# Seventeen SwiGLU pairs from seven block products: a decoder layer in split f32 on one core

## The chip, the cores and the metric

The kernel runs on one core of one Trainium2 chip. The metric is the device time of one execution in microseconds; the time of a kernel is the median of its runs. All times below are microseconds unless marked ns.

## The reference, cut to what matters

One layer (DEPTH = 1) of a decoder with D_MODEL = 1024 over 1024 prompt tokens and 32 sample tokens (8 sequences of 4), which share the weights. Two branches (a gated linear recurrence and a chunked linear attention) are merged and projected, and then comes a SwiGLU feed-forward network with D_FF = 2816, which the change touches:

```python
m = sigmoid(u_ga) * (y_a @ proj_a) + sigmoid(u_gb) * (y_b @ proj_b)
x = x + gt1 * (m @ w_out)
h2 = rmsnorm(x, norm2_g) * (1.0 + sc2) + sh2
f1, f2 = split(h2 @ ffn_w1, 2, axis=-1)          # 1024 -> 2 x 2816
x = x + gt2 * ((silu(f1) * f2) @ ffn_w2)         # 2816 -> 1024
```

All data is float32, and the result has to have float32's precision.

## The kernel before, in words

*Halves.* Half A is 512 prompt tokens; half B is the other 512 and the 32 sample tokens, 544 columns. Activations lie with features on the 128 partitions and tokens along the free axis. In half B every product is worked in two parts of 272 columns, each in its own PSUM bank of a two-bank tile from `mm(...)`.

*Split float32.* TensorE multiplies in the reduced format fp32r, so each operand is held as a high and a low part, and each 128x128 block of weights takes three matmuls: high by high (L355), high by low (L356), low by high (L357). For activations, `split` makes both parts: ACT copies the high part, DVE subtracts it. For weights, `load_raw` issues a transfer on SP's queue into a `raw` buffer (3 of them), and `split_w` splits it into an `hl` buffer (3 of them): ACT's copy L136, then DVE's subtraction L137. A split of 1024 columns serves 8 blocks.

*The feed-forward network.* D_FF is worked as 22 rows of 128 features. `pair(f, part, a)` makes one: tile `f1` (gate, 512 KB of weights, 8 blocks) and tile `f2` (value, another 512 KB), in half B 2 x 8 x 3 x 2 = 96 matmuls of 128x272. ACT takes tanh of half the gate (L1093), DVE multiplies it out (L1094, L1097), ACT and DVE split the product (L1099, L1100) into the tile `fa`, from which `ffn2` makes the output. Group 0 is pairs 0 to 10, group 1 pairs 11 to 21; `ffn2(0)` comes after group 0, `ffn2(1)` after group 1. In each half, pairs 0 to 3 are worked early, one part at a time, and from pair 4 on a pair does both parts.

*Order.* Half A runs through its branches, its attention output, second norm and FFN group 0 (all inside `branches`, the last steps in `back`), then `A.ffn1(1)` and `A.ffn2(1)`, into which half B's first norm is mixed; then half B's branches and FFN. Within that, a scheduler sets each engine's order from dependences and from priorities: what is written under `tc.high_priority(n)` goes up by n places. `split_w` has 70 (`AHEAD`). Each engine takes its instructions in its own order and waits on semaphores for the others. GpSimd (POOL) has some products of the attention, small copies of states (`hist`, `hlast`) and the issue of the output transfers (`out_ya`, `out_yb`); in the FFN it has nothing else. The tile of the tag `m2t` (one buffer of 128 x 1088) serves the recurrence of half A and then that of half B.

In the trace, tiles of half A end in `a`, those of half B in `b`: `f1psb11None` is the PSUM tile of pair 11's gate in half B.

Of the kernel before, what the change touches and what calls it, by code (L numbers as in the profile page):

```python
# [15 lines left out]
P = 128  # L16
# [4 lines left out]
NF = 22  # L21
# [6 lines left out]
LEVELS = (64, 32, 16, 8, 4, 2, 1)  # L28
EPS = 1e-6
EARLY = 4  # L30
AHEAD = 70
def starts_of(w):
    return [min(i, w - P) for i in range(0, w, P)]
# [14 lines left out]
def hybrid_layer(ctx, tc, I, O):  # L48
    nc = tc.nc
    pe, act, dve, pool, sp = nc.tensor, nc.scalar, nc.vector, nc.gpsimd, nc.sync  # L50
# [12 lines left out]
    wp = ctx.enter_context(tc.tile_pool(name="wp", bufs=3))  # L63
# [23 lines left out]
    def mm(name):  # L87
        return mmk[1].tile([P, mmk[0], 512], F32, tag="mm", name=name)
# [36 lines left out]
    def load_raw(src, n, name):  # L125
        raw = wp.tile([P, 1024], F32, tag="raw", name=name + "_raw")
        sp.dma_start(raw[:, :n], src)
        return raw

    def load_w(src, n, name):  # L130
        return split_w(load_raw(src, n, name), n, name)

    def split_w(raw, n, name):
        hl = wp.tile([P, 2, 1024], F32R, tag="hl", name=name + "_hl", bufs=3)
        with tc.high_priority(AHEAD):
            act.activation(hl[:, 0, :n], raw[:, :n], AF.Copy)  # L136
            dve.tensor_sub(hl[:, 1, :n], raw[:, :n], hl[:, 0, :n].bitcast(F32))  # L137
        return hl

    held = {}  # L140
# [17 lines left out]
    class Apart:  # L158
        def __init__(s, *of):
            s.of = of  # L160

        def __getitem__(s, at):
            rows, u, cols = at
            return s.of[u][rows, cols]

    def w_in_tile(t, name):
        return load_w(I["w_in"][t], 1024, name)

    def split(dst, src, n):
        act.activation(dst[:, 0:n], src, AF.Copy)  # L170
        dve.tensor_sub(dst[:, n:2 * n], src, dst[:, 0:n].bitcast(F32))
# [68 lines left out]
    def ada_rest():  # L240
        for cc in range(4, 12):
            yield from ada_chunk(cc)
# [45 lines left out]
    def drain(g):  # L288
        for _ in g:
            pass  # L290
# [15 lines left out]
    def mix(main, fill):  # L306
        credit = 0.0
        for want in main:
            credit = min(credit, 3.0) - want
            while credit < 0:  # L310
                got = next(fill, None)
                if got is None:
                    break
                credit += got

    class Half:
        def __init__(s, hf):
            s.hf, s.N = hf, WID[hf]
            s.n = "ab"[hf]

            s.whole = (0, s.N, None, None)
            s.parts = [(0, 256, 0, 0), (256, 256, 0, 256)] if hf == 0 else [(0, 272, 0, 0), (272, 272, 1, 0)]
            s.adas = ada_rest() if hf == 0 else iter(())
            s.early = {}
            s.lr_raw = None

        def ada(s, n):
# [728 lines left out]
        def out_proj(s, part, acc):  # L1056
            o, w = part[0], part[1]
            for q in range(KD):
# [21 lines left out]
        def pair(s, f, part, a):  # L1080
# [14 lines left out]
            p2 = mm("f2ps" + n)  # L1095
            s.gemm(p2, load_kept(("f2", f), I["ffn1"][2 * f + 1], 1024, "f2" + n, fr and f >= EARLY - 2), 8, s.h2, part=gp)
            dve.tensor_mul(ti(tg), ti(tg), s.psv(p2, part))  # L1097
# [2 lines left out]
            dve.tensor_sub(lo, tg, hi.bitcast(F32))  # L1100
            yield w * 24 / 2400.0

        def ffn1_first(s, part, n):
            for f in range(n) if part[0] == 0 else range(n - 1, -1, -1):
                if part[0] == 0:
                    s.act.append(S(f"fa{s.n}{f}", F32R))
                yield from s.pair(f, part, s.act[f])

        def ffn1(s, g, f0=0):
            if f0 == 0:  # L1110
                s.act = []
            for f in range(11 * g + f0, 11 * g + 11):
                a = S(f"fa{s.n}{f}", F32R)
                yield from s.pair(f, s.whole, a)
                s.act.append(a)
# [33 lines left out]
        def back(s):  # L1149
            s.x, s.h2 = [], []  # L1150
            p0, p1 = s.parts
            a0, a1 = [ACC("20" + s.n)], [ACC("21" + s.n)]
            drain(s.out_proj(p0, a0))
            o1 = s.out_proj(p1, a1)
            next(o1)
            next(o1)
            mix(s.norm2(p0, a0), o1)
            drain(o1)
            s.act = []
            f = s.ffn1_first(p0, EARLY)  # L1160
            next(f)
            next(f)
            mix(s.norm2(p1, a1), f)
            drain(f)
            drain(s.ffn1_first(p1, EARLY))
            drain(s.ffn1(0, EARLY))
            drain(s.ffn2(0, s.whole))

        def branches(s, before):
# [37 lines left out]
    load_later()  # L1207
    derive()
    A.branches(None)
    up1 = A.ffn1(1)  # L1210
    for _ in range(16):
        next(up1)
# [113 lines left out]
```

## Time and profile before

| what | value |
|---|---|
| median of 3 runs | 2042.29 (2042.16 to 2043.36) |
| the profiled execution, its own time | 2041.18 |
| span of its records | 2039.2 |
| granted TensorE clock, mean | 0.996 |
| busy share of the span: PE, PEld, DVE, ACT, POOL | 98%, 89%, 54%, 39%, 4% |
| moved by DMA | 228.39 MB, 112 GB/s |
| share of the 16 DMA engines taken by SP's queue | 32.8% |

A row of the timeline gives the start, the duration, the engine, the source line, the operation with its output and inputs, and in brackets how long the engine had been idle before it and what ended that. A row of the windows gives the stretch and its length, then the busy time and the count of PE, PEld, DVE, ACT and POOL, then the granted clock, the busy share of the DMA engines and the GB/s. A row of the groups by line has busy time and mean; one of the waits has who waits, who ends the wait, and sum, count and longest wait. "DMA issues" lists count, KB and microseconds from issue to landing.

### The profile page before, as it was taken

How to read it: one execution, taken by the hardware profiler on the slowest of the kernel's cores; microseconds unless marked ns; L12 is line 12 of the kernel's file. 1: busy time of each engine (PE TensorE's matmuls, PEld its weight loads, DVE VectorE, ACT ScalarE, POOL GpSimd, SP SyncE). 2: the span in 40 equal slices, each digit the busy share in tenths (PEclk: the TensorE clock that was granted, in tenths of full speed). 3: DMA queues.
4: the chain of work that ended last, by engine and by line, in shares of the span. 5: the costliest groups of instructions: out<-in, count | busy, mean ns of one | idle time of the engine just before them, and what ended most of it. 6: DMA issues, size and time to landing. Idle time of an engine off the chain costs nothing. (4 is left out here: it accounts for less than half of the span.)

```text
span 2039.2 us, 31760 instructions
## 1 busy us (share of the span) xinstructions
PE 2005.9 (98%) x13306; PEld 1808.0 (89%) x13306; DVE 1096.8 (54%) x1768; ACT 799.0 (39%) x1117; POOL 76.1 (4%) x130
## 2 busy tenths in 40 slices
PE   8999999999999999999999999999999999999997
PEld 5887877777899888888899999999999999999997
DVE  5647586544358433446473597764334773333346
ACT  3534375533335322333352355653322442222232
POOL 0101001000000000000010011010000000000000
PEclk9999999999999999999999999999999999999998
DMA  8323223334344323232412312323233542232243
GB/s 305 105 92 125 88 94 116 102 119 159 93 153 158 124 78 119 93 132 84 149 63 87 126 53 94 109 89 104 73 92 108 177 134 87 72 105 93 82 121 123
DMA packets 74638, 228.39 MB, mean 112 GB/s; under 512 B 8704, under 2 KB 16768, under 8 KB 74496
## 3 DMA queue, kind: packets, MB, share of 16 engines
q1 hardware_dynamic: 71536, 217.38, 32.8%
q0 software_dynamic: 2416, 8.44, 1.1%
q8 instruction: 104, 1.70, 0.3%
q10 hardware_dynamic: 544, 0.56, 0.1%
q14 instruction: 38, 0.31, 0.0%
HBM read 217.11 MB, written 9.23 MB: 111 GB/s over the span
## 5 line engine op out<-in xcount | busy, mean ns | idle before, releaser
L357 PE MATMUL f3psb<-fab,f3b_hl 128*128 128x272 f32 x352 | 101.4, 288 | 0.0
L355 PE MATMUL f3psb<-fab,f3b_hl 128*128 128x272 f32 x352 | 101.3, 288 | 0.0
L356 PE MATMUL f3psb<-fab,f3b_hl 128*128 128x272 f32 x352 | 100.9, 287 | 0.0
L136 ACT ACTIVATE f3b_hl<-f3b_raw 128x768 fp32r<-128x768 f32 (+1 forms) x45 | 35.7, 793 | 88.6 <-PE f3psb L357 58.3
L355 PE MATMUL f3psa<-faa,f3a_hl 128*128 128x512 f32 x176 | 68.7, 390 | 0.0
L357 PE MATMUL f3psa<-faa,f3a_hl 128*128 128x512 f32 x176 | 68.5, 389 | 0.0
L356 PE MATMUL f3psa<-faa,f3a_hl 128*128 128x512 f32 x176 | 68.5, 389 | 0.0
L355 PEld LDWEIGHTS f3psb<-fab,f3b_hl 128*128 128x128 f32 x352 | 66.4, 189 | 0.0
L357 PEld LDWEIGHTS f3psb<-fab,f3b_hl 128*128 128x128 f32 x352 | 66.2, 188 | 0.0
L356 PEld LDWEIGHTS f3psb<-fab,f3b_hl 128*128 128x128 f32 x352 | 66.1, 188 | 0.0
L137 DVE TENSOR_TENSOR f3b_hl<-f3b_raw,f3b_hl 128x768 fp32r<-128x768 f32 (+1 forms) x45 | 40.1, 892 | 35.2 <-ACT f3b_hl L136 34.8
L136 ACT ACTIVATE f3a_hl<-f3a_raw 128x768 fp32r<-128x768 f32 (+1 forms) x32 | 25.4, 793 | 84.3 <-PE f3psa L357 47.9
L137 DVE TENSOR_TENSOR f3a_hl<-f3a_raw,f3a_hl 128x768 fp32r<-128x768 f32 (+1 forms) x32 | 28.5, 892 | 39.1 <-ACT f3a_hl L136 38.4
L355 PE MATMUL uxpsb<-h1b,uxpsb_hl 128*128 128x272 f32 x160 | 47.0, 293 | 0.1
L357 PE MATMUL uxpsb<-h1b,uxpsb_hl 128*128 128x272 f32 x160 | 46.4, 290 | 0.0
L355 PE MATMUL ugpsb<-h1b,ugpsb_hl 128*128 128x272 f32 x160 | 46.2, 289 | 0.0
L357 PE MATMUL ugpsb<-h1b,ugpsb_hl 128*128 128x272 f32 x160 | 46.1, 288 | 0.0
L356 PE MATMUL uxpsb<-h1b,uxpsb_hl 128*128 128x272 f32 x160 | 45.9, 287 | 0.0
L356 PE MATMUL ugpsb<-h1b,ugpsb_hl 128*128 128x272 f32 x160 | 45.8, 286 | 0.0
L357 PEld LDWEIGHTS f3psa<-faa,f3a_hl 128*128 128x128 f32 x176 | 33.0, 188 | 7.0 <-DVE f3a_hl L137 0.2
L356 PEld LDWEIGHTS f3psa<-faa,f3a_hl 128*128 128x128 f32 x176 | 33.0, 188 | 6.9
L355 PEld LDWEIGHTS f3psa<-faa,f3a_hl 128*128 128x128 f32 x176 | 33.0, 188 | 6.8
(1477 smaller groups left out, 7129.0 us busy)
## 6 DMA issues: line engine op xcount, KB each, us to landing
ada<-in_ada_w SPq DMA_DIRECT2D x48, 512.0 KB, 5.3
f3b_raw<-in_ffn SPq DMA_DIRECT2D x23, 384.0 KB, 3.1
f3b_raw<-in_ffn SPq DMA_DIRECT2D x22, 320.0 KB, 2.9
woa_raw<-in_w_out SPq DMA_DIRECT2D x13, 512.0 KB, 3.5
wob_raw<-in_w_out SPq DMA_DIRECT2D x13, 512.0 KB, 3.2
f3a_raw<-in_ffn SPq DMA_DIRECT2D x16, 384.0 KB, 3.1
uxpsa_raw<-in_w_in SPq DMA_DIRECT2D x10, 512.0 KB, 3.6
ugpsa_raw<-in_w_in SPq DMA_DIRECT2D x10, 512.0 KB, 3.6
```

Of the source, the lines that this page charges most:

```text
L136: act.activation(hl[:, 0, :n], raw[:, :n], AF.Copy)
L137: dve.tensor_sub(hl[:, 1, :n], raw[:, :n], hl[:, 0, :n].bitcast(F32))
L355: pe.matmul(out, wh, x[:, o:o + w], start=st, stop=False)
L356: pe.matmul(out, wh, x[:, N + o:N + o + w], start=False, stop=False)
L357: pe.matmul(out, wl, x[:, o:o + w], start=False, stop=en)
```

## The change

*Fewer products.* A pair of half B has two outputs (gate f1 and value f2) for two parts of 272 tokens, from two halves of the 1024 features (k-tiles 0 to 3 and 4 to 7): as blocks, a 2x2 matrix times a 2x2 matrix, eight block products of 4 blocks and 12 matmuls each. For pairs 5 to 21, `pair7` makes the four outputs from seven such products, after Strassen and Winograd, with sums of the weights on the one side and of the tokens on the other. With A0, A1 for the gate's weights and B0, B1 for the value's (0: k-tiles 0 to 3, 1: 4 to 7), and h for the first part's tokens:

- x = A0 h (tile `qa`, first 512 columns), and later, called x' here, A1 h is added to it in the same bank (`qa`, second half): the gate of the first part;
- y = d0 t2 and v = d2 t3 (tile `qc` holds d0 and d2);
- z = d3 t1, and B1 t4 is added to v (tile `qb` holds d3 and B1);
- d1 times the second part's k-tiles 4 to 7 is added to z (tile `qd`, only 512 wide).

d0 = A0+B0+B1, d1 = d0+A1, d2 = A0+B0, d3 = B0+B1. Results x and y share the PSUM tile `xy`, v and z the tile `wz`. Between the products, `e` is ACT's copy of x ahead of x', u2 = y - e (L1189), u4 = u2 + v (L1194); the value f2 of the second part is u4 - z (L1201), that of the first u2 + v (L1203), and the gate of the second part z - u2 (L1208). Its tanh (L1209), L1210, the product with f2 over 544 columns (L1211) and the split (L190, L191) finish the pair. Tiles `qa` and `qc` are split by ACT and DVE as before (now L137, L138); for `qb` and `qd` GpSimd subtracts the low part. A pair takes six transfers of 256 or 512 KB on SP's queue instead of two of 512 KB, and 84 matmuls instead of 96.

*The sums of the weights.* `make_sums` runs after half A's branches: for each of the 17 pairs two rounds on GpSimd, each with two loads of 256 KB on its own queue, four additions of 128x256, and a store of 512 KB into a DRAM tile `sum`. All rounds use the one buffer of the tag `m2t`.

*The sums of the tokens.* `mixed` runs in half B between pair 4 and pair 5: from h2's 8 tiles it makes t1 to t4, for each of four j eight DVE additions or subtractions of 272 or 544 columns and three splits. t1 takes the place of the second part in h2's tiles 0 to 3, the others have tiles of their own.

```diff
-    def split_w(raw, n, name):
+    def split_w(raw, n, name, eng=None):
...
-            dve.tensor_sub(hl[:, 1, :n], raw[:, :n], hl[:, 0, :n].bitcast(F32))
+            (eng or dve).tensor_sub(hl[:, 1, :n], raw[:, :n], hl[:, 0, :n].bitcast(F32))
...
+    def make_sums(fs):
+        for f in fs:
+            sums[f] = dp.tile([P, 4, 512], F32, tag=f"sum{f}", name=f"sum{f}")
+            for i in range(2):
+                q = tp.tile([P, 2 * 544], F32, tag="m2t", name=f"sq{f}{i}", bufs=1)[:, :1024].rearrange("p (s n) -> p s n", s=4)
+                c = slice(256 * i, 256 * i + 256)
+                for u in range(2):
+                    pool.dma_start(q[:, 2 * u:2 * u + 2, :], I["ffn1"][2 * f + u].rearrange("p (k n) -> p k n", k=2)[:, :, c])
+                pool.tensor_add(q[:, 3], q[:, 2], q[:, 3])
+                pool.tensor_add(q[:, 2], q[:, 0], q[:, 2])
+                pool.tensor_add(q[:, 0], q[:, 0], q[:, 3])
+                pool.tensor_add(q[:, 1], q[:, 1], q[:, 0])
+                pool.dma_start(sums[f][:, :, c], q)
...
+        def mixed(s):
+            N, w = s.N, s.N // 2
+            s.t1, s.t2, s.t3, s.t4 = [], [], [], []
+            for j in range(4):
+                n = f"{s.n}{j}"
+                h, g = s.h2[j], s.h2[4 + j]
+                hs, gs = T("mh" + n), T("mg" + n)
+                dve.tensor_add(hs[:, :N], h[:, :N].bitcast(F32), h[:, N:2 * N].bitcast(F32))
+                dve.tensor_add(gs[:, :N], g[:, :N].bitcast(F32), g[:, N:2 * N].bitcast(F32))
+                p, q = T("mp" + n), T("mq" + n)
+                dve.tensor_sub(p[:, :w], hs[:, :w], hs[:, w:N])
+                dve.tensor_add(p[:, w:N], p[:, :w], gs[:, w:N])
+                dve.tensor_sub(q[:, :w], hs[:, w:N], gs[:, w:N])
+                dve.tensor_sub(q[:, w:N], gs[:, :w], p[:, w:N])
+                t34 = S("mt" + n, F32R)
+                split(t34, q[:, :N], N)
...
+                split(t2[:, c:c + N], p[:, w:N], w)
...
+                hi, lo = h[:, w:N], h[:, N + w:2 * N]
+                act.activation(hi, p[:, :w], AF.Copy)
+                dve.tensor_sub(lo, p[:, :w], hi.bitcast(F32))
...
+        def pair7(s, f, a):
...
+            xy, wz = mm("xy" + n), mm("wz" + n)
+            x, y = (xy[:, 0, :w], xy[:, 1, :w]) if s.hf else (xy[:, 0, :w], xy[:, 0, w:N])
+            v, z = (wz[:, 0, :w], wz[:, 1, :w]) if s.hf else (wz[:, 0, :w], wz[:, 0, w:N])
...
+            ha = load_w(I["ffn1"][2 * f], 1024, "qa" + n)
+            prod(x, ha, 0, s.quarter(0, 0), True, True)
+            with tc.high_priority(AHEAD + 20):
+                act.activation(e, x, AF.Copy)
+            hc = load("qc", (d[:, 0], d[:, 2]))
+            prod(y, hc, 0, s.t2, True, True)
+            with tc.high_priority(AHEAD + 20):
+                dve.tensor_sub(u2, y, e)
+            prod(x, ha, 1, s.quarter(4, 0), False, True)
+            prod(v, hc, 1, s.t3, True, True)
+            with tc.high_priority(AHEAD + 20):
+                dve.tensor_add(u4, u2, v)
+            act.activation(tg[:, :w], x, AF.Tanh, scale=0.5)
+            dve.scalar_tensor_tensor(tg[:, :w], tg[:, :w], 1.0, x, op0=OP.add, op1=OP.mult)
+            hb = load("qb", (d[:, 3], I["ffn1"][2 * f + 1][:, 512:]), pool)
+            prod(z, hb, 0, s.t1, True, True)
+            with tc.high_priority(AHEAD + 20):
+                dve.tensor_sub(f2[:, w:N], u4, z)
+            prod(v, hb, 1, s.t4, False, True)
+            dve.tensor_add(f2[:, :w], u2, v)
+            hd = load("qd", (d[:, 1],), pool)
+            prod(z, hd, 0, s.quarter(4, 1), False, True)
+            with tc.high_priority(AHEAD + 20):
+                dve.tensor_sub(f12, z, u2)
+            act.activation(tg[:, w:N], f12, AF.Tanh, scale=0.5)
+            dve.scalar_tensor_tensor(tg[:, w:N], tg[:, w:N], 1.0, f12, op0=OP.add, op1=OP.mult)
+            dve.tensor_mul(tg[:, :N], tg[:, :N], f2[:, :N])
+            split(a, tg[:, :N], N)
...
-                yield from s.pair(f, s.whole, a)
+                yield from s.pair7(f, a) if s.seven and f >= PLAIN else s.pair(f, s.whole, a)
...
     A.branches(None)
+    make_sums(range(PLAIN, NF))
```

Lines of `pair7`, `mixed` and `make_sums` are counted in the changed kernel, where L355 to L357 of a seven-product pair are L1166 to L1168.

*How the order moves.* First TensorE in half B, at the seam in a pair: before, the last matmuls of pair 5's gate and the first of its value (`f1psb5None`, `f2psb5None`).

```order
L355 MATMUL f1psb5None_14851<-h2b_14088,f1b5None_hl 128x272
L356 MATMUL f1psb5None_14851<-h2b_14088,f1b5None_hl 128x272
L357 MATMUL f1psb5None_14851<-h2b_14088,f1b5None_hl 128x272
L355 MATMUL f2psb5None_14908<-h2b_13975,f2b5None_hl 128x272 [waits DVE_49,Activation_49]
L356 MATMUL f2psb5None_14908<-h2b_13975,f2b5None_hl 128x272
L357 MATMUL f2psb5None_14908<-h2b_13975,f2b5None_hl 128x272 [waits DVE_49]
```

After, the last matmul of y (weights `qc`, tokens `mu`, that is t2), the last of v's first product (tokens `mt`, t3), and the first five of x', for the pair after the first.

```order
L1168 MATMUL xyb_15338<-mub_15189,qcb_hl 128x272
L1168 MATMUL wzb_15339<-mtb_15204,qcb_hl 128x272
L1166 MATMUL xyb_15338<-h2b_14325,qab_hl 128x272 [waits DVE_49]
L1167 MATMUL xyb_15338<-h2b_14325,qab_hl 128x272
L1168 MATMUL xyb_15338<-h2b_14325,qab_hl 128x272
```

Before, TensorE waits here for the split of weights that has been asked for ahead; now x' goes into the tile of which y has just been written, and its first matmul waits for the DVE instruction that reads y, L1189. A product of the next pair (x) is also moved in between this pair's: the order of products is z of `qb`, half of the next x, v of t4, the other half but one matmul, z of `qd`, that matmul, v of t3, y and x'.

DVE at the same place, before: splits of weights (L137), and one pair's gating (L1094, L1097, L1100).

```order
L1100 TENSOR_TENSOR fab_14735<-ftb4None_14790,fab_14735 128x544
L1094 SCALAR_TENSOR_TENSOR ftb5None_14905<-ftb5None_14905,f1psb5None_14851 128x544
L137 TENSOR_TENSOR f2b6None_hl<-f2b6None_raw,f2b6None_hl 128x1024
L1097 TENSOR_TENSOR ftb5None_14905<-ftb5None_14905,f2psb5None_14908 128x544
L137 TENSOR_TENSOR f1b7None_hl<-f1b7None_raw,f1b7None_hl 128x1024
L1100 TENSOR_TENSOR fab_14850<-ftb5None_14905,fab_14850 128x544
```

After: the split of `qc`, the last steps of the pair before (tiles `vf`, `tg`, `ff`, `fa`; numbers 15211 to 15217), and u2 of this pair (`eu`, 15340).

```order
L138 TENSOR_TENSOR qcb_hl<-qcb_raw,qcb_hl 128x1024
L1208 TENSOR_TENSOR vfb_15215<-wzb_15213,eub_15214 128x272
L1210 SCALAR_TENSOR_TENSOR tgb_15216<-tgb_15216,vfb_15215 128x272
L1211 TENSOR_TENSOR tgb_15216<-tgb_15216,ffb_15217 128x544
L1189 TENSOR_TENSOR eub_15340<-xyb_15338,eub_15340 128x272
L191 TENSOR_TENSOR fab_15211<-tgb_15216,fab_15211 128x544
L1194 TENSOR_TENSOR vfb_15341<-eub_15340,wzb_15339 128x272
L138 TENSOR_TENSOR qab_hl<-qab_raw,qab_hl 128x1024
L1201 TENSOR_TENSOR ffb_15343<-vfb_15341,wzb_15339 128x272
```

L1189, for which x' waits, stands in DVE's queue behind L1208, L1210 and L1211 of the pair before, which follow z and ACT's tanh.

GpSimd in half A, before: the last copies of states, then the transfers of A's output.

```order
L899 COPY hist<-uba_3137 128x3
L953 COPY hlast<-laa_3239 128x1
L953 COPY hlast<-laa_3255 128x1
L1147 DMA out_ya<-ya_7652 128x1024
L1147 DMA out_ya<-ya_7656 128x1024
L1147 DMA out_ya<-ya_7660 128x1024
```

After, at the same place: the first round of sums (`sq` is the work buffer, `sum` the DRAM tile).

```order
L179 DMA sq_6273<-in_ffn 128x2x256
L974 COPY hlast<-laa_3241 128x1
L179 DMA sq_6273<-in_ffn 128x2x256
L974 COPY hlast<-laa_3257 128x1
L180 TENSOR_TENSOR sq_6273<-sq_6273 128x256
L181 TENSOR_TENSOR sq_6273<-sq_6273 128x256
L182 TENSOR_TENSOR sq_6273<-sq_6273 128x256
L183 TENSOR_TENSOR sq_6273<-sq_6273 128x256
L184 DMA sum_6272<-sq_6273 512x1x256
```

Thirty-three more rounds follow, and the transfers of `out_ya` stand behind the last store:

```order
L183 TENSOR_TENSOR sq_6553<-sq_6553 128x256
L184 DMA sum_6544<-sq_6553 512x1x256
L1259 DMA out_ya<-ya_7943 128x1024
L1259 DMA out_ya<-ya_7947 128x1024
L1259 DMA out_ya<-ya_7951 128x1024
```

More of the change, by code (lines that the diff above doesn't have):

```diff
@@ L30 @@
 EARLY = 4
+PLAIN = 5
 AHEAD = 70
@@ L164, in __getitem__ @@
             return s.of[u][rows, cols]
+    dp = ctx.enter_context(tc.tile_pool(name="dp", bufs=1, space=bass.MemoryType.DRAM))
+    sums = {}
+    def make_sums(fs):
[11 more added lines that the diff above has]
+                pool.dma_start(sums[f][:, :, c], q)
     def w_in_tile(t, name):
@@ L324, in __init__ @@
             s.early = {}
+            s.seven = s.hf == 1
             s.lr_raw = None
@@ new lines, in quarter, with prod, load @@
+        def quarter(s, k0, c):
+            N, w = s.N, s.N // 2
+            return [(h[:, c * w:c * w + w], h[:, N + c * w:N + c * w + w]) for h in s.h2[k0:k0 + 4]]
+        def pair7(s, f, a):
+            n, N, w = f"{s.n}{f}", s.N, s.N // 2
+            d = sums[f]
+            def prod(out, hl, u, rhs, first, last):
+                for k, (xh, xl) in enumerate(rhs):
+                    c = u * 512 + k * P
+                    wh, wl = hl[:, 0, c:c + P], hl[:, 1, c:c + P]
+                    pe.matmul(out, wh, xh, start=(first and k == 0), stop=False, skip_group_check=True)
+                    pe.matmul(out, wh, xl, start=False, stop=False, skip_group_check=True)
+                    pe.matmul(out, wl, xh, start=False, stop=(last and k == 3), skip_group_check=True)
+            def load(name, parts, eng=None):
+                raw = wp.tile([P, 1024], F32, tag="raw", name=name + n + "_raw")
+                for i, src in enumerate(parts):
+                    sp.dma_start(raw[:, i * 512:(i + 1) * 512], src)
+                return split_w(raw, 512 * len(parts), name + n, eng)
+            xy, wz = mm("xy" + n), mm("wz" + n)
+            x, y = (xy[:, 0, :w], xy[:, 1, :w]) if s.hf else (xy[:, 0, :w], xy[:, 0, w:N])
+            v, z = (wz[:, 0, :w], wz[:, 1, :w]) if s.hf else (wz[:, 0, :w], wz[:, 0, w:N])
+            eu, vf, tg, f2 = T("eu" + n), T("vf" + n), T("tg" + n), T("ff" + n)
+            e, u2 = eu[:, :w], eu[:, w:N]
+            u4, f12 = vf[:, :w], vf[:, w:N]
+            ha = load_w(I["ffn1"][2 * f], 1024, "qa" + n)
[6 more added lines that the diff above has]
+                dve.tensor_sub(u2, y, e)
+            yield w * 24 / 2400.0
+            prod(x, ha, 1, s.quarter(4, 0), False, True)
[4 more added lines that the diff above has]
+            dve.scalar_tensor_tensor(tg[:, :w], tg[:, :w], 1.0, x, op0=OP.add, op1=OP.mult)
+            yield w * 24 / 2400.0
+            hb = load("qb", (d[:, 3], I["ffn1"][2 * f + 1][:, 512:]), pool)
[4 more added lines that the diff above has]
+            dve.tensor_add(f2[:, :w], u2, v)
+            yield w * 24 / 2400.0
+            hd = load("qd", (d[:, 1],), pool)
[6 more added lines that the diff above has]
+            split(a, tg[:, :N], N)
+            yield w * 12 / 2400.0
@@ L1165, in back @@
             drain(s.ffn1_first(p1, EARLY))
-            drain(s.ffn1(0, EARLY))
+            f = s.ffn1(0, EARLY)
+            if s.seven:
+                for _ in range(2 * (PLAIN - EARLY)):
+                    next(f)
+                s.mixed()
+            drain(f)
             drain(s.ffn2(0, s.whole))
```

7 lines of the change are left out of this document (added).

## The prediction

> **What bounds the kernel now.** I read the page's first two parts, then the busy time by stage, then the starts of the pairs in half B's FFN.
>
> ```profile
> span 2039.2 us, 31760 instructions
> PE 2005.9 (98%) x13306; PEld 1808.0 (89%) x13306; DVE 1096.8 (54%) x1768; ACT 799.0 (39%) x1117; POOL 76.1 (4%) x130
> ...
> PEclk9999999999999999999999999999999999999998
> ```
>
> ```profile
> 537.00:760.00 223.00, 222.66 (x1349) 199.85 (x1348) 119.05 (x196) 82.67 (x125) 0.00 (x0) 1.00 0.40 126
> 1689.00:1763.00 74.00, 74.00 (x597) 74.00 (x596) 27.80 (x32) 19.95 (x26) 0.00 (x0) 1.00 0.24 77
> 1827.00:1958.00 131.00, 131.00 (x1055) 131.00 (x1054) 48.88 (x57) 33.92 (x43) 0.00 (x0) 1.00 0.26 87
> ```
>
> ```profile
> L355 PE MATMUL f1psb11None<-h2b,f1b11None_hl x16: 285/287/287, 1826.9 to 1832.5; 128*128 128x272 f32 x16
> L355 PE MATMUL f1psb21None<-h2b,f1b21None_hl x16: 285/287/287, 1946.4 to 1952.0; 128*128 128x272 f32 x16
> ```
>
> TensorE is busy for 98% of the span at the full clock, and in the FFN stages of half B for every microsecond, with DVE and ACT at about a third and GpSimd at zero. Ten pairs start in 1946.4 - 1826.9 = 119.5 us: 11.95 us for 96 matmuls, a pitch of 0.1245 us. (The 0.29 us of one record is its latency.) So time goes only if matmuls go, and comes back wherever TensorE has to wait. A block product is 12 matmuls, 1.494 us.
>
> **The change part by part.**
>
> *Removed.* 17 pairs x 12 matmuls x 0.1245 = 25.4 us of TensorE work; a pair that never waits would take 84 x 0.1245 = 10.46 us.
>
> *Added waits.* Durations and hand-offs, from pairs before the change:
>
> ```profile
> 1844.71 0.29 PE L357 MATMUL f1psb12None<-h2b,f1b12None_hl 128*128 128x272 f32 x1
> 1845.04 0.62 ACT L1093 ACTIVATE ftb12None<-f1psb12None 128x544 f32<-128x544 f32 x1 [4.37 <-PE f1psb12None L357]
> 1845.56 1.05 ACT L136 ACTIVATE f2b13None_hl<-f2b13None_raw 128x1024 fp32r<-128x1024 f32 x1
> 1846.64 1.23 DVE L137 TENSOR_TENSOR f2b13None_hl<-f2b13None_raw,f2b13None_hl 128x1024 fp32r<-128x1024 f32 x1 [0.23 <-ACT f2b13None_hl L136]
> 1840.16 1.22 DVE L137 TENSOR_TENSOR f1b13None_hl<-f1b13None_raw,f1b13None_hl 128x1024 fp32r<-128x1024 f32 x1 [0.37 <-ACT f1b13None_hl L136]
> 1841.30 0.72 DVE L1100 TENSOR_TENSOR fab<-ftb11None,fab 128x544 fp32r<-128x544 f32 x1
> 1677.78 0.44 DVE L1097 TENSOR_TENSOR ftb<-ftb,f2psb 128x272 f32<-128x272 f32 x1 [0.38 <-PE f2psb L357]
> 1674.79 0.40 ACT L1093 ACTIVATE ftb<-f1psb 128x272 f32<-128x272 f32 x1 [1.56 <-PE f1psb L357]
> ...
> 38.80 1.23 DVE L137 TENSOR_TENSOR early_hl<-early_raw,early_hl 128x1024 fp32r<-128x1024 f32 x1 [7.63 <-ACT early_hl L136]
> 40.08 0.19 PEld L357 LDWEIGHTS early<-h1a,early_hl 128*128 128x128 f32 x1 [0.89 <-DVE early_hl L137]
> 40.08 0.50 PE L357 MATMUL early<-h1a,early_hl 128*128 128x512 f32 x1 [0.46 <-DVE early_hl L137]
> 40.42 0.39 PE L355 MATMUL early<-h1a,early_hl 128*128 128x512 f32 x1
> ```
>
> A consumer starts 0.04 us after the record it waits for ends. A 1024-wide split costs ACT 1.06 and DVE 1.23; 544 columns cost DVE 0.72, 272 columns 0.44 (ACT 0.40); the next instruction of DVE or ACT starts some 0.09 before the record ends (1.23 but 1.14 to the next start). A TensorE that had to wait restarts with its weight load: 0.34 instead of 0.23 to the next matmul, 0.11 lost each time.
>
> Now one steady pair, in the order of the new program: z(qb) 12 matmuls, x of the next pair 6, v(t4) 12, x 5, z(qd) 12, x 1, v(t3) 11, y 12, v 1, x' 12. Each two-bank tile holds two results, and TensorE's next write into one waits for the reader of the other.
>
> 1. The next pair's first tile qa takes the buffer that x' just left. From the end of x' (record 0.165 past the pitch): 0.04 + 1.06 + 0.04 + 1.23 + 0.04 + 0.11 = 2.69 us until the third x matmul, which reads the low part, can run; TensorE arrives after 14 matmuls, 1.74. Wait 0.94.
> 2. z(qd) waits until DVE has read v: 0.165 + 0.04 + 0.44 + 0.15 = 0.79, with 5 matmuls (0.62) between: 0.16. Two more waits, for ACT's copy of x behind a 1024-wide split, and for qc: 0.25 together.
> 3. x' waits for u2 = y - e on DVE. DVE's queue has, ahead of u2, the last gating steps of the pair before (272 and 544 wide, all operands in SBUF), and these wait for ACT's tanh. Counted from the end of z(qd): the split of qb can start then (its buffer is qd's), so ACT ends it at 1.27; the copy of x and the tanh follow to 1.93. GpSimd starts its half of that split at 1.31. What GpSimd does to DVE is in the trace:
>
> ```profile
> 69.12 2.40 POOL L647 TENSOR_TENSOR qea<-qa,e0a 128x1024 f32<-128x1024 f32 x1 [47.88 <-ACT e0a L646]
> 71.49 3.39 POOL L655 TENSOR_TENSOR kea<-kea,ka 128x1024 f32<-128x1024 f32 x1
> 68.97 1.29 DVE L664 TENSOR_TENSOR atta<-dpsa,ident 128x512 f32<-128x512 f32 x2
> 70.18 2.44 DVE L137 TENSOR_TENSOR vpsa_hl<-vpsa_raw,vpsa_hl 128x1024 fp32r<-128x1024 f32 x1
> 72.54 2.89 DVE L694 TENSOR_TENSOR wa<-bca 128x512 f32<-128x512 f32 x1
> 75.35 0.68 DVE L695 TENSOR_TENSOR wa<-bca 128x512 f32<-128x512 f32 x1
> ```
>
> The 1024-wide split that takes 1.23 alone took 2.44: it ended 1.1 after GpSimd's 2.40 us product (to 71.52). The 512-wide subtraction (0.68 alone) took 2.89, held until GpSimd's next ended. The instructions with one operand in PSUM (x2, 1.29) passed. So GpSimd's 1024-wide subtraction of qb, 2.40 us, holds DVE's gating until 3.71; then 0.43, 0.72 and u2 0.44 with their hand-offs end at 5.25, and TensorE restarts at 5.40. It arrives after 25 matmuls and the waits between, 3.36. Wait 2.05.
>
> The row shows this of TENSOR_TENSOR; the first gating step is a SCALAR_TENSOR_TENSOR, and no run here shows one held. [...]
>
> Sum of a pair's waits: 0.94 + 0.16 + 0.25 + 2.05 = 3.4; the pair takes 13.9 instead of 11.95. Ends: 2.0 if GpSimd held nothing (u2 then follows y, wait 0.7), and 4.4 if GpSimd's subtraction takes the 3.39 of the second row, which itself began held. I take 2.40, the row that ran alone. This counts for pairs 6 to 10 and 12 to 21: 15 x 3.4 = 51 us.
>
> *The first seven-product pair.* Between pair 4's last product and pair 5's x', DVE has 10 instructions of 544 columns (0.63 apart) and 19 of 272 (0.35): 12.9 us, plus 2.4 held by pair 5's own GpSimd split, plus u2 and hand-offs 0.8: 16.1. TensorE has 36 matmuls, 4.5 us, in that time: 12 us of wait (9 without the hold, 14 at most). Around ffn2, pair 10's last product and pair 11's start wait some 2 us more.
>
> *The clock.*
>
> ```profile
> PE rpsoa L374 <- DVE atta L664: 3.5, 1, 3.5
> PE spsb L710 <- DVE wb L701: 2.3, 1, 2.3
> ```
>
> ```profile
> 174.00:176.00 2.00, 1.66 (x9) 1.66 (x9) 2.00 (x4) 1.06 (x1) 0.00 (x0) 0.65 0.04 14
> 176.00:178.00 2.00, 2.00 (x12) 0.75 (x11) 1.81 (x3) 1.08 (x2) 0.00 (x0) 0.50 0.00 0
> 1182.00:1184.00 2.00, 0.95 (x16) 0.98 (x16) 2.00 (x4) 2.00 (x3) 0.00 (x0) 1.00 0.00 0
> ```
>
> The 3.5 us wait ended at 174.3, and the granted clock was then 0.65 and 0.50; after the 2.3 us wait it stayed at 1.00. The waits in the first pair reach 3 us with little between: 2 us for half clock (0 to 4). Seam waits of 2.05 should not cost any.
>
> *GpSimd's sums in half A.*
>
> ```profile
> 476.93 1.68 POOL L953 COPY hlast<-laa 128x1 f32<-128x1 f32 x2 [62.45 <-DVE laa L951]
> 1009.00 0.59 POOL L1147 DMA_DIRECT2D out_ya<-ya  x1 [530.39 <-DVE ya L1144]
> 1028.46 3.38 POOL L647 TENSOR_TENSOR qeb<-qb,e0b 128x1088 f32<-128x1088 f32 x1 [14.95 <-ACT e0b L646]
> ```
>
> ```profile
> out_ya<-ya POOLq DMA_DIRECT2D x4, 512.0 KB, 3.7
> out_yb<-yb POOLq DMA_DIRECT2D x4, 272.0 KB, 4.1
> ```
>
> The work buffer is A's recurrence tile, free at about 477; in GpSimd's queue the last sum stands ahead of the out_ya transfers, needed at 1009. 34 rounds fit if each takes under (1009 - 477) / 34 = 15.6 us. A round: two issues (0.6 each), a load of 256 KB (4.1, by the 272 KB row with similar runs), four adds at 2.40 / 4 = 0.6 (2.6, up to 4 with DVE's holds), an issue, a 512 KB store (3.7 to 5): 12.6, between 11 and 15. It fits, ending near 905. The 136 adds hold DVE now and then; DVE is busy 119 of 223 us there and only the second norm gates TensorE: 2 us (0 to 5). SP issues six transfers a pair instead of two; with two to three microseconds to spare by the waits above, they are taken at nothing: what covers them is the slower pair itself.
>
> *Sum*, against the profiled execution (2041.2, of which 2039.2 is span): 2041.2 - 25.4 + 51 + 12 + 2 + 2 + 2 = 2084.8. The median of the runs is 1.1 above that execution: **2086 us**, 2.1% slower.
>
> **The rivals.**
>
> *Every seam wait is covered* (faster): TensorE stays as packed as the rows of before show it, because DVE and ACT are two thirds idle. Then 2041.2 - 25.4 + 12 + 2 + 2 + 1.1 = 2033. Decides when a pair's waits stay under (25.4 - 18) / 15 = 0.5 us. Against it: wait 1 alone is 0.94, from two durations that are quoted above. 6 in 100; a partial cover near no change, 3 in 100.
>
> *GpSimd does not hold the gating.* Waits 2.0 a pair: 2086 - 15 x 1.35 - 2.4 - 2 = 2061. Against it stand the 2.44 and 2.89. 7 in 100.
>
> *The clock gate closes at each seam*: with 3 us at half clock a pair, 1.5 lost: 2086 + 22 = 2108. [...] This case decides if a seam's wait passes 3. 8 in 100.
>
> *The sums come late*: at 17 us a round they end at 1055, and half B's first GpSimd product (1028) and the output tiles wait: some 35 us more, 2121. 7 in 100.
>
> **How the numbers follow.** The forecast has 69 in 100, with its own range 2068 to 2104 (waits of 2.4 to 4.4 a pair, first pair 9 to 14). The range 2055 to 2116 adds the seam without a hold and the closed clock, and leaves out the covered seams, the late sums and the far tails of the forecast, 2 in 10. A change under 0.2% (4 us) cannot be told here. Slower 0.91, same 0.03, faster 0.06.
>
> **What would show it.** Pair starts (tile xyb) 13.9 us apart, not 10.5 or 12.5; TensorE waiting about 2 us before x' for DVE's L1189, and 0.9 at the third x matmul for L138; DVE's L1210 recorded at 2 us or more while GpSimd's L138 runs; about 12 us of waits ahead of pair 5's x'; granted clock 1.00 from pair 6 on; the last sum stored before 960. Pairs under 11 us apart, or GpSimd's L138 far from 2.4, would make the forecast wrong.

## The result and the profile after

The changed kernel took 2095.91 us (median of 4 runs, 2094.43 to 2097.18) beside 2042.82 for the kernel before: a ratio of 1.0254, with a 95% interval of 1.0236 to 1.0273. The forecast was 2086, range 2055 to 2116. The profiled execution took 2094.43, with a span of 2092.7, 53.5 longer than before. The runs of one kernel spread over up to 13 us in this study (the kernel before on one chip: 2038 to 2051), the longer ones at a lower mean clock (0.991 beside 0.997). First the page's span and engines, and the clock in 40 slices:

```profile
span 2092.7 us, 32080 instructions
PE 2010.7 (96%) x13102; PEld 1796.6 (86%) x13102; DVE 1193.7 (57%) x1906; ACT 841.3 (40%) x1197; POOL 329.7 (16%) x402
...
PEclk9999999999999999999999999999999989999999
```

TensorE idles for 82 us instead of 33, and the clock's row has an 8 in the 33rd slice (1674 to 1726), in which the first seven-product pair lies. The waits of TensorE in half B's FFN (who, for whom, sum, count, longest):

```profile
PE xyb L1166 <- DVE eub L1189: 25.3, 15, 1.7
PE xyb L1168 <- DVE qab_hl L138: 9.6, 15, 0.7
PE wzb L1166 <- ACT mtb L190: 4.0, 3, 2.3
PE wzb L1167 <- DVE mtb L191: 3.8, 3, 2.5
```

Fifteen times x' waits for u2 (L1189), 25.3 in all, and fifteen times the third x matmul for qa's low part, 9.6: the two seam waits of the forecast. The chain of one pair, each row released by the one ahead of it:

```profile
1889.69 1.06 ACT qbb_hl L137
1890.75 0.29 ACT eub L1185
1891.04 0.33 ACT tgb L1209
1891.39 2.13 DVE tgb L1210
1893.54 0.72 DVE tgb L1211
1894.27 0.36 DVE eub L1189
1894.67 0.39 PE xyb L1166
...
1896.47 1.07 ACT qab_hl L137
1897.56 1.24 DVE qab_hl L138
1898.84 0.40 PE xyb L1168
```

Down to the last row this is the forecast's steps 3 and 1: ACT's split of qb, the copy of x, the tanh, a gating step of 2.12 us, the product, u2, x'; then qa's split, which x' had kept out of its buffer, and the third x matmul. Why L1210 takes 2.12 stands in the timeline of the same place:

```profile
1890.83 2.38 POOL L138 TENSOR_TENSOR qbb_hl<-qbb_raw,qbb_hl 128x1024 fp32r<-128x1024 f32 x1 [7.76 <-ACT qbb_hl L137]
1891.39 2.12 DVE L1210 SCALAR_TENSOR_TENSOR tgb<-tgb,vfb 128x272 f32<-128x272 f32 x1 [1.30 <-ACT tgb L1209]
...
L1189 DVE TENSOR_TENSOR eub<-xyb,eub x10: 431/433/434, 1880.4 to 2004.7; 128x272 f32<-128x272 f32 x10
```

L1210 starts at 1891.39, and instead of 0.43 it lasts until 0.3 after GpSimd's subtraction ends (1893.21). Ten u2 lie in steps of (2004.7 - 1880.4) / 9 = 13.81 us.

Two places where time went that the forecast had small. In half A (groups of one tile by start: before, after) and in half B's attention:

```profile
L355 PE MATMUL f1psa4None<-h2a,f1a4None_hl x8: 389/389/396, 674.3 to 679.0; 128*128 128x512 f32 x8
L376 PE MATMUL f1psa4None<-h2a,f1a4None_hl x8: 389/389/396, 684.4 to 689.2; 128*128 128x512 f32 x8
```

```profile
626.00:690.00 64.00, 58.44 (x431) 56.23 (x430) 47.48 (x84) 27.88 (x48) 25.67 (x30) 0.95 0.65 215
1306.00:1316.00 10.00, 9.24 (x41) 8.00 (x41) 6.28 (x15) 5.62 (x9) 0.00 (x0) 0.66 0.46 170
1708.00:1720.00 12.00, 7.50 (x26) 6.12 (x27) 11.06 (x26) 4.36 (x9) 0.00 (x0) 0.50 0.11 33
```

Pair 4 of half A starts 10.1 later than before; the windows' column after the five engines is the granted clock, 0.95 there, 0.66 at 1306 to 1316, in which half B's own work is unchanged, and 0.50 in the first seven-product pair.

### The profile page after: what moved, and what is told of

Read it like the earlier page. It is cut to its first block, busy times and chain, and to the rows that moved or that the text cites. A ratio compares the mean times of both kernels' runs of the same rounds, so it can differ in the third digit from the quotient of the medians.

```text
span 2092.7 us, 32080 instructions
## 1 busy us (share of the span) xinstructions
PE 2010.7 (96%) x13102; PEld 1796.6 (86%) x13102; DVE 1193.7 (57%) x1906; ACT 841.3 (40%) x1197; POOL 329.7 (16%) x402
## 5 line engine op out<-in xcount | busy, mean ns | idle before, releaser
L138 POOL TENSOR_TENSOR qbb_hl<-qbb_raw,qbb_hl 128x1024 fp32r<-128x1024 f32 x17 | 40.5, 2381 | 402.5 <-DVE mpb L1135 214.4
L179 POOL DMA_DIRECT2D sq<-in_ffn x68 | 48.2, 716 | 181.5 <-DMA sum<-sq 115.3
L1166 PE MATMUL xyb<-h2b,qab_hl 128*128 128x272 f32 x136 | 41.3, 304 | 25.3 <-DVE eub L1189 25.3
L137 ACT ACTIVATE f3b_hl<-f3b_raw 128x768 fp32r<-128x768 f32 (+1 forms) x45 | 35.6, 794 | 74.5 <-PE f3psb L378 54.7
L138 DVE TENSOR_TENSOR f3b_hl<-f3b_raw,f3b_hl 128x768 fp32r<-128x768 f32 (+1 forms) x45 | 40.0, 892 | 34.0 <-ACT f3b_hl L137 33.8
L137 ACT ACTIVATE f3a_hl<-f3a_raw 128x768 fp32r<-128x768 f32 (+1 forms) x32 | 25.4, 795 | 83.9 <-PE f3psa L378 47.5
L138 DVE TENSOR_TENSOR f3a_hl<-f3a_raw,f3a_hl 128x768 fp32r<-128x768 f32 (+1 forms) x32 | 29.6, 926 | 38.9 <-ACT f3a_hl L137 38.3
L1166 PEld LDWEIGHTS xyb<-h2b,qab_hl 128*128 128x128 f32 x136 | 26.0, 191 | 28.8 <-DVE eub L1189 28.8
L1168 PE MATMUL xyb<-h2b,qab_hl 128*128 128x272 f32 x136 | 40.9, 301 | 9.6 <-DVE qab_hl L138 9.6
L376 PE MATMUL uxpsb<-h1b,uxpsb_hl 128*128 128x272 f32 x160 | 47.5, 297 | 0.1
L378 PE MATMUL uxpsb<-h1b,uxpsb_hl 128*128 128x272 f32 x160 | 46.5, 291 | 0.0
L376 PE MATMUL ugpsb<-h1b,ugpsb_hl 128*128 128x272 f32 x160 | 46.2, 289 | 0.0
L378 PE MATMUL ugpsb<-h1b,ugpsb_hl 128*128 128x272 f32 x160 | 46.1, 288 | 0.0
```

The lines of the kernel that those rows point to most:

```text
L138: (eng or dve).tensor_sub(hl[:, 1, :n], raw[:, :n], hl[:, 0, :n].bitcast(F32))
L179: pool.dma_start(q[:, 2 * u:2 * u + 2, :], I["ffn1"][2 * f + u].rearrange("p (k n) -> p k n", k=2)[:, :, c])
L376: pe.matmul(out, wh, x[:, o:o + w], start=st, stop=False)
L378: pe.matmul(out, wl, x[:, o:o + w], start=False, stop=en)
L1166: pe.matmul(out, wh, xh, start=(first and k == 0), stop=False, skip_group_check=True)
L1168: pe.matmul(out, wl, xh, start=False, stop=(last and k == 3), skip_group_check=True)
```

## The experiments

Because of that spread, places are compared in the profiles, and times by ratios to the kernel before, run beside each kernel on the same chip.

**1. The sums alone.** Every pair takes eight products; the sums are made and not used.

```diff
-            s.seven = s.hf == 1
+            s.seven = False
```

> The weight sums are made in half A, but every pair of half B takes its eight products from the plain weights, so only the sums' own cost is left. Theory: TensorE in half A waits where the 10.1 us were seen after the change (around the second norm, 626 to 684 us), for DVE steps held by GpSimd's additions and for transfers of xra that came late; with the half clock that follows, 10 us: 2052 (2050 to 2055), with pair 4's gate of half A at about 684 instead of 674. Rival: the waits are the ones of before, and a half clock that came by chance made the 10 us; then 2042 to 2046.

Ratio 1.0054 (1.0037 to 1.0070), 11 us, median 2057.47; the profiled execution took 2050.40. Pair 4's gate of half A and the waits around the norm:

```profile
L376 PE MATMUL f1psa4None<-h2a,f1a4None_hl x8: 389/389/396, 683.7 to 688.5; 128*128 128x512 f32 x8
...
PE f1psa L376 <- ACT h2a L455: 1.9, 1, 1.9
```

In this execution every place from there to the end stays 9.3 to 9.5 behind: its loss is all at the second norm, and it is the sums'. The median lies above the expected 2050 to 2055; where the other executions lost more than the profiled one, no profile shows.

**2. Seven products without sums.** The slices d0 to d3 are plain weights, loaded from where the weights lie.

```diff
-            d = sums[f]
+            w1, w2 = I["ffn1"][2 * f], I["ffn1"][2 * f + 1]
+            d = [w1[:, :512], w1[:, 512:], w2[:, :512], w2[:, 512:]]
...
-    make_sums(range(PLAIN, NF))
```

> The pairs of half B are made from seven products as changed, with the same transfers and instructions, but the four 512-wide tiles that stand for the sums are loaded straight from the weights (so the values are not the sums), and nothing is summed in half A. Theory: half A is as before (pair 4's gate at 674), half B as changed (13.8 us a pair): 2094.4 - 10 = 2084 (2081 to 2087). Rival: half B's transfers from the sums' DRAM tiles are what is late; then reading from the weights moves the pairs as well, under 13 us, 2070 or less.

This kernel leaves out the sums, so its result is not the layer's. Median 2084.35, ratio 1.0188 (1.0170 to 1.0207), as expected. Half A is back (674.9), and u2's steps are (1997.9 - 1873.5) / 9 = 13.82: the store in DRAM and GpSimd's work in half A do nothing to the pairs.

```profile
L376 PE MATMUL f1psa4None<-h2a,f1a4None_hl x8: 389/389/396, 674.9 to 679.7; 128*128 128x512 f32 x8
...
L1190 DVE TENSOR_TENSOR eub<-xyb,eub x10: 434/434/434, 1873.5 to 1997.9; 128x272 f32<-128x272 f32 x10
```

**3. DVE subtracts all low halves.**

```diff
-            hb = load("qb", (d[:, 3], I["ffn1"][2 * f + 1][:, 512:]), pool)
+            hb = load("qb", (d[:, 3], I["ffn1"][2 * f + 1][:, 512:]))
...
-            hd = load("qd", (d[:, 1],), pool)
+            hd = load("qd", (d[:, 1],))
```

> DVE subtracts the low halves of qb and qd as well, GpSimd has nothing to do in the pairs. Theory (GpSimd's subtraction holds DVE's gating): L1210 falls from 2.12 to about 0.43 us and the wait for L1189 before x' from 1.7 to about 0.5, although DVE has 1.7 us more to do in each pair; pairs 12.6 us apart instead of 13.8; 2094.4 - 16 x 1.2 - 2 = 2073 (2069 to 2079). Rival (DVE's own queue makes u2 late): the added splits stand ahead of u2 as well, the wait stays at 1.7 or grows; 2095 to 2110.

Median 2077.31, ratio 1.0156 (1.0133 to 1.0179), as expected.

```profile
L1210 DVE SCALAR_TENSOR_TENSOR tgb<-tgb,vfb x10: 433/434/435, 1876.5 to 1990.1; 128x272 f32<-128x272 f32 x10
L1189 DVE TENSOR_TENSOR eub<-xyb,eub x10: 432/433/434, 1877.6 to 1991.3; 128x272 f32<-128x272 f32 x10
...
PE xyb L1166 <- DVE eub L1189: 8.1, 15, 0.5
```

L1210 takes 0.43, u2's wait falls from 25.3 to 8.1 for fifteen pairs, and the step is 113.7 / 9 = 12.63. DVE has 1.7 more to do in each pair and is still faster: the time was GpSimd's hold, not DVE's load.

**4. Other tiles.**

```diff
-            xy, wz = mm("xy" + n), mm("wz" + n)
+            xv, yz = mm("xv" + n), mm("yz" + n)
...
+            x, v = xv[:, 0, :w], xv[:, 1, :w]
+            y, z = yz[:, 0, :w], yz[:, 1, :w]
```

> x shares its two-bank PSUM tile with v, and y with z, instead of x with y and v with z; nothing else is changed. Theory: x' waits for u2 only because y, which u2 reads, lies in the tile that x' writes; with v there it has only to wait for ACT's copy of x. The 1.7 us go, GpSimd's hold stays (L1210 at 2.1 us), and qa's and qc's splits are waited for instead: pairs 12.7 us apart, 2094.4 - 16 x 1.1 = 2077 (2072 to 2083). Rival (what u2 needs is late, whatever the tile): some other product waits the same time for the same chain, pairs stay at 13.8, 2090 to 2097.

Median 2067.92, ratio 1.0113 (1.0098 to 1.0128): a larger gain than expected, and the rival is out. Of the 9 us under the forecast, 16 x 0.3 = 4.8 are the step (12.4 in place of 12.7). Another 2.9 are, by the author's estimate, the half clock in half B's attention of the changed kernel's profile: the last u2 lies 26.2 earlier here (1978.5 in place of 2004.7), and the steps make 16 x 1.4 = 22.4 of that.

```profile
L1210 DVE SCALAR_TENSOR_TENSOR tgb<-tgb,vfb x11: 434/1785/1975, 1865.2 to 1987.7; 128x272 f32<-128x272 f32 x11
L1189 DVE TENSOR_TENSOR eub<-yzb,eub x11: 426/434/439, 1854.4 to 1978.5; 128x272 f32<-128x272 f32 x11
...
PE xvb L1168 <- DVE qab_hl L138: 11.9, 15, 1.0
PE yzb L1168 <- DVE qcb_hl L138: 4.9, 15, 0.3
...
1879.89 0.66 ACT L190 ACTIVATE fab<-tgb 128x544 fp32r<-128x544 f32 x1 [2.60 <-DVE tgb L1211]
1881.14 1.06 ACT L137 ACTIVATE qab_hl<-qab_raw 128x1024 fp32r<-128x1024 f32 x1
```

GpSimd still holds L1210 (1.8), but nothing waits for u2: the step is 124.1 / 10 = 12.4, and what is waited for are the low parts of qa (11.9 for fifteen) and qc (4.9). So x' waited for the held chain only since it shared a tile with y. (With the tiles the scheduler's order moved as well: v of t3 now follows x'.) The hold may still have a part in the 11.9: in the last two rows ACT waits 2.60 for L1211, which follows the held L1210, and its copy of qa stands behind that, 1.6 after x' had ended (1879.56). No run has these tiles without the hold and with the old order of the low-weight matmuls. Experiments 3 and 4 each take a link out of the same chain, and bring 1.2 and 1.4 of a pair's 3.35.

**5. The sums' transfers without their additions** (eight products in every pair; the four `pool.tensor_add` lines of `make_sums` are left out).

> As the run with the sums alone (eight products in every pair), but the four additions of each round are left out: GpSimd only issues the loads and the stores. Theory: the 9.4 us lost around half A's second norm are GpSimd's additions holding DVE; without them nothing is lost, 2042 to 2044, pair 4's gate of half A at 674 to 676. Rival: the additional traffic makes xra and the weights late; then most of the 9.4 stays, 2048 to 2053, gate at 680 to 684.

Ratio 1.0023 (1.0009 to 1.0036), median 2049.88. Neither was right alone: the time is in the rival's range, but pair 4's gate starts at 677.9, between the two; it is 3.7 late, where experiment 1 had 9.4.

```profile
L372 PE MATMUL f1psa4None<-h2a,f1a4None_hl x8: 389/389/396, 677.9 to 682.7; 128*128 128x512 f32 x8
...
629.73 0.48 DVE L1069 SCALAR_TENSOR_TENSOR xma<-wopsa,gains,xra 128x256 f32<-128x256 f32 x1 [1.94 <-DMA xra<-in_xa]
631.40 0.38 PE L374 MATMUL f1psa<-h2a,f1a_hl 128*128 128x256 f32 x1 [1.03 <-DVE f1a_hl L138]
```

The residual xra lands late (DVE waits 1.94 for it, 0.61 before the change), TensorE waits 1.03 for a split of weights behind that step and then 0.89 for ACT, and TensorE then ran at half clock for a while (0.57 over 632 to 636, 0.88 over 626 to 640), which makes the rest of 3.7. By the ratios the transfers alone cost 4.7 us and all of it 11; by these two gates, 3.7 and 9.4. So the additions make rather more than half. The share is not exact: how late that gate is differs between executions with the sums (7.0 to 12.8 in six of them), and without additions the rounds follow one another faster, so that more was moved just ahead of the norm (258 GB/s over 600 to 626, 204 in experiment 1).

**6. Group 1 only.** `PLAIN = 11`: eleven pairs, token sums made under ffn2(0).

> PLAIN is 11 instead of 5: only the eleven pairs of group 1 take seven products, and the token sums are made while TensorE works at ffn2(0), which needs DVE little. Nothing else differs from the changed kernel. Theory: what group 0 cost, 18.2 us (10.5 of waits and half clock in the first pair, 5 x 1.85 for the others, less 1.5), goes, and pair 11 begins without a wait of more than 3 us; the norm of half A still loses 9.4; 2075 (2071 to 2080). Rival: the token sums are as late at pair 11 as at pair 5, since the splits of f3's weights stand ahead of them in DVE's queue; 2083 to 2090.

Median 2072.59, ratio 1.0137 (1.0114 to 1.0159), as expected.

```profile
L376 PE MATMUL f3psb<-fab,f3b_hl x352: 283/287/395, 1768.1 to 2052.4; 128*128 128x272 f32 x176
...
PE xyb L1166 <- DVE eub L1189: 16.9, 10, 1.7
```

The waits for the token sums (`mtb`) are gone from the list, and eleven pairs wait for u2 ten times. ffn2 begins at 1768.1, 6.9 later than before the change, and half A was 7.0 late in this execution: group 0 costs nothing now, and pair 11 begins without a wait for token sums.

**7. Three mends.** All seventeen pairs; the edits of 3 and 4, and the four low-weight matmuls of each product last:

```diff
-                    wh, wl = hl[:, 0, c:c + P], hl[:, 1, c:c + P]
+                    wh = hl[:, 0, c:c + P]
...
-                    pe.matmul(out, wl, xh, start=False, stop=(last and k == 3), skip_group_check=True)
+                for k, (xh, xl) in enumerate(rhs):
+                    c = u * 512 + k * P
+                    pe.matmul(out, hl[:, 1, c:c + P], xh, start=False, stop=(last and k == 3), skip_group_check=True)
```

> All seventeen pairs, with three edits of the seam together: DVE's subtractions instead of GpSimd's, x with v and y with z in a tile, and in each product the four low-weight matmuls last instead of one in each three. Theory: the three waits of a pair go one by one (hold, shared tile, low half of the weights), what stays is 0.6 us: pairs 11.1 us apart, under the 11.95 of eight products; with the first pair's 10.5 and half A's 9.4 as they are, 2049 (2044 to 2055). Rival: some other chain (ACT's splits, SP's six transfers) bounds a pair above 11.95; 2062 or more.

Median 2053.84, ratio 1.0045 (1.0028 to 1.0062): as expected. The step is (1961.6 - 1848.3) / 10 = 11.3, under eight products' 11.95. At the end the profile is 11.0 behind the one before, and 9.5 of that was lost by pair 4 of half A; the first pair's waits (for `mub`) eat what the other pairs bring. The order of the low-weight matmuls was not run by itself, so what it brings alone is not shown; the waits for the low parts of qa and qc, which experiment 4 had, are gone.

```profile
L1191 DVE TENSOR_TENSOR eub<-yzb,eub x11: 431/433/441, 1848.3 to 1961.6; 128x272 f32<-128x272 f32 x11
...
PE yzb L1166 <- ACT mub L190: 5.8, 3, 4.4
```

**8. The mended kernel.** The three mends, `PLAIN = 11`, and the 22 rounds of sums held back until pair 4 of half A has its result (`make_sums(range(PLAIN, NF), A.act[4])`):

```diff
+                if f == fs[0] and i == 0:
+                    pool.tensor_copy(q[:, 0, :1], after[:, :1].bitcast(F32))
```

> The three mends of the seam, seven products in group 1 only (token sums under ffn2(0)), and the weight sums, now 22 rounds, begun only after pair 4 of half A, by a copy of one column from that pair's result into the work buffer. Theory: half A loses nothing (the sums run from 686 to about 980, before 1009), eleven pairs at 11.1 instead of 11.95 bring 9 us, the hand-over to ffn2 takes 1 to 3 back: 2035 (2030 to 2040), faster than both. Rival: the sums' additions hold something in half A's later stages as well, or the token sums come late: 2042 to 2050.

> The mended kernel once more, beside the one with the sums in two parts: 2037 to 2041, and 2 to 3 us slower than that one; the first lrpsb of half B at 995 to 996.

Ratios 0.9983 (0.9970 to 0.9997) and, the second time, 0.9989 (0.9977 to 1.0000); medians 2039.43 and 2041.24. Slightly faster than before the change (the second interval reaches to no change), by less than the 7 expected; the second median lies just above its range. In the first profile pair 4 of half A is on time (674.4) and the pairs are at 11.24, but the rival had its part: the last sum is stored at 968.7, and half B's first norm, in which DVE is busy for 23.4 of 24 us (946 to 970), then waits.

```profile
L1193 DVE TENSOR_TENSOR eub<-yzb,eub x11: 433/433/442, 1834.6 to 1947.0; 128x272 f32<-128x272 f32 x11
...
PE f3psa L380 <- DVE f3a_hl L138: 2.1, 2, 1.9
L563 PEld LDWEIGHTS lrpsb<-h1b,lr_hlb x16: 186/188/192, 995.9 to 1000.7; 128*128 128x128 f32 x16
```

The first `lrpsb` is 2.6 late (995.9; before 993.3). In the second profile it starts at 993.5, not at the expected 995 to 996, but there pair 4 of half A starts early as well, at 672.0, after shorter waits in the first 400 us. Counted from pair 4 it is 321.5 both times, and 319.0 before the change: the same loss.

**9. Sums in two parts.** The first eight rounds start at once, the other 14 after pair 4 (`f == fs[4]` in the line above).

> As the mended kernel, but the weight sums of the first four pairs are made as soon as the buffer is free, and only the other 14 rounds wait for pair 4 of half A. Theory: of the mended kernel's rounds the last came at 969 us, into half B's first norm (946 to 970), where DVE was busy for all of the time and f3a's split was waited for, 2.6 us; with eight rounds before 585 and the others from 686 to about 875, neither norm meets an addition, half A's gate of pair 4 is at 674 and half B's first lrpsb at 993 as before the change, and the time is 2.5 us under the mended kernel's. Rival: the 2.6 us were not the additions' doing; then the two kernels are the same.

Ratio 0.9971 (0.9957 to 0.9985), median 2038.31, against 2041.24 for the mended kernel beside it; the fastest run took 2033.42. The last sum is stored at 860.7, `lrpsb` starts at 993.0, and neither norm is late (pair 4 of half A at 674.1, and from there to `lrpsb` 318.9): 2.9 less by the medians (expected 2.5). The two ratios' intervals overlap, so the 2.6 is shown by the places rather than by the times. It is 0.3% faster than the kernel before, and by both ratios 2.8% faster than the changed one.

```profile
L186 POOL DMA_DIRECT2D sum<-sq x22: 750/752/752, 487.4 to 860.7; - x22
L563 PEld LDWEIGHTS lrpsb<-h1b,lr_hlb x16: 186/188/192, 993.0 to 997.7; 128*128 128x128 f32 x16
```

## Why the prediction was right, term by term

The direction, the mechanism and the range held; the time was 9.9 over the forecast. By the starts of tiles in the two traces:

| term | forecast | measured |
|---|---|---|
| 17 x 12 matmuls removed | -25.4 | -25.4 |
| seam waits of 15 pairs | 15 x 3.4 = 51 | 15 x (13.81 - 10.46) = 50.3 |
| first pair and its half clock | 12 + 2 | 13.2 |
| around both ffn2, with pair 11's own start | 2 | 2.5 |
| half A | 2 | 10.1 |
| half clock in half B's attention | none | 2.9 |
| sum | 43.6 | 53.6 |

*Half A was mis-sized*, the largest error. The step was "the 136 adds hold DVE now and then ... only the second norm gates TensorE: 2 us". The place was right, the price was not. In the timeline of before and of after, the same three steps of that norm:

```profile
629.65 1.27 DVE L421 SCALAR_TENSOR_TENSOR xn2a<-xma,gains,rb2a 128x256 f32<-128x256 f32 x3
631.55 0.48 DVE L1073 SCALAR_TENSOR_TENSOR xma<-wopsa,gains,xra 128x256 f32<-128x256 f32 x1 [1.51 <-DMA xra<-in_xa]
632.99 0.77 POOL L180 TENSOR_TENSOR sq<-sq 128x256 f32<-128x256 f32 x1 [4.65 <-DMA sq<-in_ffn]
633.83 0.79 POOL L181 TENSOR_TENSOR sq<-sq 128x256 f32<-128x256 f32 x1
633.96 2.68 DVE L442 SCALAR_TENSOR_TENSOR xn2a<-xma,gains,rb2a 128x256 f32<-128x256 f32 x3
```

L442's three instructions took 2.68 instead of 1.27, while GpSimd's additions ran one after another beside them (in experiment 5, without additions, the same three took 1.27); they had begun late, after xra, for which DVE waited 1.51 (0.61 before). TensorE's waits from 600 to 700 come to 6.4, the longest 2.0, and the clock fell (0.95 over 64 us), which the forecast had priced in half B only. Experiment 1 shows the sum, 5 that transfers and additions both have a part. The upper end of this term, 5, was too low as well: the prediction had the 34 rounds' transfers only as a question of whether they fit, not as traffic beside xra.

*The seam* was right, wait by wait. The waits listed, u2's 25.3 / 15 = 1.7 and qa's 0.64, count from the end of the record before, 0.165 past the pitch, and without the 0.11 of a restart. By the starts of the matmuls of one pair (1894.67 to 1908.46), u2 cost 1.96 (forecast 2.05), qa 0.94 (0.94), z of `qd` 0.18 (0.16) and the two short waits 0.26 (0.25): 3.34 in place of 3.4. That the first gating step, a SCALAR_TENSOR_TENSOR, would be held, on which the 2.05 rests, no run had shown ahead of the result; it was held: 2.12 with GpSimd's subtraction beside it, 0.43 without (experiment 3). The rival without a hold gave waits of 2.0; experiment 3, in which there is none, has 12.63 - 10.46 = 2.2. That x' need not wait for u2 at all (experiment 4) the prediction did not consider: it took the shared tile as given.

*The first pair* waited 7.8 in six listed waits, with half the clock from 1708 to 1720 (0.50). From its first matmul (1702.5) to pair 6's x' (1734.0) are 31.5 us for 120 matmuls of 0.1245; less pair 6's own 3.35 that is 13.2 over a pair that never waits, forecast 14. (In `mixed`, each j has six additions or subtractions and three splits on DVE, not eight and three.) The hold there is in the trace as forecast: one of the 272-wide instructions of `mixed` (L1136) took 2.62 while GpSimd split qb.

```profile
1703.91 2.35 POOL L138 TENSOR_TENSOR qbb_hl<-qbb_raw,qbb_hl 128x1024 fp32r<-128x1024 f32 x1 [214.40 <-DVE mpb L1135]
1703.93 2.62 DVE L1136 TENSOR_TENSOR mpb<-mpb,mgb 128x272 f32<-128x272 f32 x1
```

*Around ffn2* TensorE lost 1.6 from pair 10's x' to pair 12's, beyond pair 12's own 3.35, and after pair 21's x' 0.9 more than the kernel before at its end: 2.5, forecast 2. Pair 11 is rightly not among the 15: its u2 ran as soon as y was done (1865.7), and x' lost only 0.14.

*The sums* were in time, as forecast: the last was stored at 926 (forecast 905), 13.2 us a round (12.6).

*Nothing spoke for the clock closing at the seams*: it stayed at 1.00 from 1730 on, with seam waits of up to 1.96. That a seam's wait has to pass 3 for it was the author's estimate, between the 2.3 and the 3.5 of the rows before; no run shows where it lies, nor the 3 us at half clock a pair. In the first pair, where the listed waits of up to 2.5 follow one another, the clock was 0.50.

## What to carry to other kernels

Fewer products pay only if the seam between them is as tight as before: here each pair saved 1.49 us and lost 3.35 to a chain of short steps on the other engines. Two of its links could each be shortened by one edit alone (the helper engine's hold, two results in one tile), and together with a third edit (the low weights asked for later) a pair came below eight products. Work on an idle engine was not free here: it held a busy one (L1210 took 2.12 in place of 0.43), and its transfers delayed another's (DVE waited 1.51 for xra in place of 0.61). Look for the stages in which the busy engine gates TensorE, and place the helper's work between them. Preparations (the token sums) belong under a stage that leaves their engine free, where they cost nothing here (experiment 6).

## What the runs showed of the hardware that was not expected

The clock halved or not at one and the same place, in one execution and not in another. In half B's attention, TensorE has 3.2 us of one-column matmuls and two short waits (0.26 and 0.49). Before the change and after it, the second ten of them and what follows:

```profile
1298.41 1.28 PE L362 MATMUL opsb<-ones,oacb 128*128 128x1 f32 x10 [0.49 <-DVE oacb L841]
1308.26 2.29 PE L383 MATMUL opsb<-ones,oacb 128*128 128x1 f32 x10 [0.49 <-DVE oacb L862]
1310.41 2.16 PE L943 MATMUL g1b<-xcb,lwb_raw 128*128 128x272 f32 x4
```

The instructions and their waits (0.49) are the same, but after the change the second ten took 2.29 instead of 1.28, and the next group 2.16 (1.16 before); 3.1 us were lost in all (2.9 in the table above, since a wait just ahead was 0.2 shorter). The granted clock was 0.50 from 1310 to 1314, and 0.66 over 1306 to 1316; before the change it was 1.00 at that place (1296 to 1306).

It was 0.66 as well in the second profile of the mended kernel and 0.70 in that of the sums in two parts (1296 to 1306 in both). In experiment 1, whose kernel differs nowhere ahead of that place from the changed one, the second ten took 1.28 and the next group 1.16. The first profile of the mended kernel has no such loss either: from `lrpsb` to ffn2's first matmul it takes 768.7 us, the kernel before 767.9, the second profile 772.9. What decides it, no run here shows. Though TensorE is busy by the profile at these matmuls of one column, the clock fell there in three of these six executions.
